# A hybrid Hyena and attention layer on one core: the RMSNorm sums taken by one product of ones with the squares

## The chip, the core and the metric

The kernel runs on one core of one Trainium2 chip. The metric is the device time of one execution in microseconds, the median over the runs. The engines are called PE (matrix products), DVE, ACT, POOL (three elementwise engines) and SP (which issues most DMAs).

## What is computed

One encoder layer on 512 positions of width 1024, all float32:

```python
def rmsnorm(x, g):
    return x * rsqrt(mean(x * x, axis=-1) + 1e-6) * g

x = x + 0.5 * swiglu(rmsnorm(x, ffn1_norm_g), ...)            # first FFN, width 2816
P = rmsnorm(x, mix_norm_g) @ w_in                             # 3*512 Hyena + 3*512 attention columns
y = concat(rmsnorm(hyena(P), g_h), rmsnorm(attention(P), g_a))
x = x + y @ w_out
x = x + 0.5 * swiglu(rmsnorm(x, ffn2_norm_g), ...)            # second FFN ("the second layer")
out = rmsnorm(x, final_norm_g)
```

So there are six norms: before the first FFN, before the mixer, on the Hyena output, on the attention output, before the second FFN, and the final one.

## The kernel before, in words

Activations lie transposed: a tile is 128 channels x 512 positions, so `g.x[0..7]` are the eight tiles of x, and a norm's sum runs over the partitions and over the tiles. Every large product is made of three matmuls of 128x128 by 128x512 (`mm3`, lines 146 to 148): high part by high part, low by high, high by low. The high and low parts of an activation tile are made by `gained`: ACT writes the high part times the norm's gain (tile `xh`, line 235), DVE the rest (`xl`, line 236). Weights are split in the same way by `wh` on ACT (line 188) and `wl` on DVE (line 194). A norm's factor does not go into the product's input; it multiplies the result, as a tile `rb` of 128x512 that holds 1/rms of each position in every row.

`SumSq.add` squares a tile on ACT (lines 249 and 252, tiles `ssq` and `sq`) and adds it to the sum on POOL (line 256). `SumSq.rstd` then turns the sum into `rb`: four products of 128 columns of the sum with a column of ones give the sums as 128x4 (`pc`, line 267); ACT takes the root (`std`, line 271, a table load ahead of it where another function was loaded), DVE the reciprocal (`rc`, line 273); DVE puts it on the diagonal of four 128x128 blocks (`dg`, line 276); PE multiplies by ones (`pb`, line 280); ACT copies that to SBUF (`rb`, line 285).

The stages: the first FFN (`ffn`, with its products `pgu` and `pd`); the mixer (`Mixer`: projections `pp` and `pv`, FFT-like products, elementwise work on DVE) and attention (`Attention`: `pqk`, softmax, `ppt`, `po`); the output projection in `Attention.out` (`pw`, eight output tiles, first with the Hyena half, then with the attention half); the second FFN; the final norm, which is worked off in two halves of 256 positions in `tail`. In the output projection's second half `evac` works off each tile d: `wt` = `pw` times the attention norm's `rb` (line 1047), x = x + `wt` (line 1049), the square of x through `done(d)`, and then `gained`, which gives `xh` and `xl` of the second FFN. The second FFN's first product needs all eight `xh` and `xl`.

The order on each engine is set twice. The code's streams are generators that a planner (`Merge`) lets run by estimated costs (`on_p`, `on_v`, `on_a`, `wait`); that gives the order in which instructions are written. The framework's own scheduler then puts them in the order in which each engine has them, within the dependencies and the ring buffers. The engines work in that order.

Of the kernel before, what the change touches and what calls it, by code (L numbers as in the profile page):

```python
# [18 lines left out]
P = 128  # L19
S = 512  # L20
# [46 lines left out]
def wait(ev):  # L67
    return "W", ev
# [172 lines left out]
class SumSq:  # L241
# [16 lines left out]
    def rstd(self, n, lag, res, m, ev=None, keep=True):  # L258

        g, nc = self.g, self.g.nc  # L260
        yield on_v(0.0, lag)
        yield on_p(1.7, ps=1)
        pc = psum(g, "pc")
        parts = [t for t in (self.acc, self.last) if t is not None]
        for b in range(4):
            for i, t in enumerate(parts):
                nc.tensor.matmul(pc[:, b:b + 1], t[:, b * P:(b + 1) * P], g.ones[:, 0:1],
                                 start=i == 0, stop=i == len(parts) - 1)
        yield on_v(0.7, 2.0)
# [12 lines left out]
        if keep:  # L282
            yield on_v(0.0, 0.9)
            res["rb"] = g.wp.tile([P, S], F32, tag="rb", name="rb", bufs=1)
            nc.scalar.copy(res["rb"], pb)
            m.free(ps=1)
        if ev is not None:
            m.fire(ev)

# [404 lines left out]
class Mixer:  # L694


    def __init__(self, g, m, hp, mid, xg):
        self.g, self.m, self.hp, self.mid, self.xg = g, m, hp, mid, xg
        self.conv = {}
        self.nev, self.gev = Event(), Event()  # L700
# [56 lines left out]
    def vproj(self):  # L757
# [15 lines left out]
        yield wait(self.nev)  # L773
# [101 lines left out]
class Attention:  # L875
# [146 lines left out]
    def out(self, done):  # L1022
# [15 lines left out]
        def evac(d, ps, last):  # L1038
# [11 lines left out]
            done(d)  # L1050
# [3 lines left out]
            self.x2[d] = gained(g, g.x[d], NG2 + d)  # L1054

        self.wev, self.x2 = Event(), [None] * DT
        for part in range(2):
            yg = self.yag if part else yhg
            for d in range(DT):
# [20 lines left out]
def body(ctx: ExitStack, tc: tile.TileContext, a: dict, out: bass.AP):  # L1080
# [83 lines left out]
    with pool("m1", **over) as hp:  # L1164
# [4 lines left out]
        m.spawn(ssm.rstd(D, LM, g.nm, m, mx.nev), 0)  # L1169
# [8 lines left out]
        def done(d):  # L1178
            ss2.add(g.x[d])

        m.spawn(at.prep_qk(), PQ)
        m.spawn(at.out(done), 20)
# [7 lines left out]
    with pool("f2", **over) as fp:  # L1190
# [12 lines left out]
        def tail(d, th, ps):  # L1203
# [3 lines left out]
            if d == DT - 2:  # L1207
                yield on_p(0.4, 0.0, ps=1)
# [12 lines left out]
            yield on_p(0.3)  # L1221
# [5 lines left out]
            yield on_v(0.3, 0.6)  # L1227
            std = g.wp.tile([P, 4], F32, tag="std", name="std", bufs=2)
# [142 lines left out]
```

## Time and profile before

| | us |
|---|---|
| runs | 1066.83, 1072.60, 1072.99 |
| median | 1072.6 |
| the profiled execution | 1065.19 |
| its span, first to last instruction | 1063.4 |
| mean granted clock of PE in it | 0.992 of full |

Rows of the profile give for each group of instructions the line, the engine, output<-inputs, partitions x elements and the count; a row of the timeline starts with its start and its duration, and ends with the idle time before it and what ended that. Instructions of an engine overlap somewhat, so a duration is about 0.08 us longer than the distance to the next one on DVE. A float32 product (`pc`, `pb`) is two instructions in the trace. PEclk is the granted clock as a share of full speed, where 1.00 is 2.4 GHz and 0.50 is 1.2 GHz.

### The profile page before, as it was taken

To read this page: it belongs to the slowest core of one execution; us is meant where nothing else is said; L and a number is where in the kernel's file an instruction comes from. 1 tells how busy PE (TensorE), PEld (TensorE's weight loads), DVE (VectorE), ACT (ScalarE), POOL (GpSimd) and SP (SyncE) were. 2 spreads that over 40 slices of the span, in tenths; PEclk is the share of its full clock that TensorE was granted. 3 is DMA by queue.
4 is the path that set the end of the run, shared out by engine and by line. 5 is a ranking of instruction groups with operands and counts; after the bars stand their busy time and mean duration, and the time that the engine had idled before them with its cause. 6 is when DMAs were issued, how large, how long until landed. Compare 5 with 4: busy or idle time off the path is not lost.

```text
span 1063.4 us, 12596 instructions
## 1 busy us (share of the span) xinstructions
PE 1046.8 (98%) x4962; PEld 860.2 (81%) x4962; DVE 609.3 (57%) x856; ACT 404.5 (38%) x598; POOL 45.1 (4%) x37
## 2 busy tenths in 40 slices
PE   9999999999999999999998999999999999999996
PEld 7877888888888888888886978688888888888886
DVE  5577646555666454879999355944444334444333
ACT  6433432234234342354348773432322122322341
POOL 4000000000000120000000100400000000000010
PEclk9999999999999999999999999899999999999998
DMA  6333324532264222334444303122222223333222
GB/s 213 118 132 104 124 89 137 163 97 90 90 192 156 89 98 70 98 100 144 163 131 153 94 1 99 55 84 99 99 99 100 86 93 99 99 100 99 85 74 80
DMA packets 43512, 114.25 MB, mean 107 GB/s; under 512 B 5081, under 2 KB 12313, under 8 KB 43452
## 3 DMA queue, kind: packets, MB, share of 16 engines
q1 hardware_dynamic: 41644, 111.30, 32.1%
q10 hardware_dynamic: 1808, 2.14, 0.6%
q8 instruction: 39, 0.64, 0.3%
q14 instruction: 21, 0.17, 0.0%
HBM read 106.08 MB, written 7.34 MB: 107 GB/s over the span
## 4 chain that ended last, share of the span: by engine, by line
PE 93%; DVE 3%; ACT 1%; DMA 1%; issue 1%; SPq 0%; DVEq 0%; ACTq 0%
PE pgu L148 15%; PE pgu L147 15%; PE pgu L146 15%; PE pd L146 8%; PE pd L147 8%; PE pd L148 8%; PE pp L146 3%; PE pp L148 3%; PE pp L147 3%; PE po L978 2%; PE pqk L994 1%; PE ppt L969 1%; PE pw L146 1%; PE pw L148 1%; PE pw L147 1%
## 5 line engine op out<-in xcount | busy, mean ns | idle before, releaser
L188 ACT ACTIVATE wh<-wr 128x1024 fp32r<-128x1024 f32 x159 | 168.5, 1060 | 431.9 <-PE pgu L147 139.7
L147 PE MATMUL pgu<-xl,wh 128*128 128x512 f32 x704 | 276.4, 393 | 2.8 <-DVE xl L236 2.7
L146 PE MATMUL pgu<-xh,wh 128*128 128x512 f32 x704 | 276.9, 394 | 0.6 <-ACT wh L556 0.6
L148 PE MATMUL pgu<-xh,wl 128*128 128x512 f32 x704 | 276.1, 392 | 0.2
L194 DVE TENSOR_TENSOR wl<-wr,wh 128x1024 fp32r<-128x1024 f32 x159 | 196.8, 1238 | 104.0 <-ACT wh L188 101.0
L147 PEld LDWEIGHTS pgu<-xl,wh 128*128 128x128 f32 x704 | 133.1, 189 | 33.4 <-DVE xl L236 4.8
L146 PEld LDWEIGHTS pgu<-xh,wh 128*128 128x128 f32 x704 | 132.8, 189 | 31.8 <-issue 2.9
L148 PEld LDWEIGHTS pgu<-xh,wl 128*128 128x128 f32 x704 | 133.1, 189 | 28.9 <-DVE wl L194 0.6
L146 PE MATMUL pd<-gh,wh 128*128 128x512 f32 (+1 forms) x374 | 143.2, 383 | 0.0
L147 PE MATMUL pd<-gl,wh 128*128 128x512 f32 (+1 forms) x374 | 142.7, 382 | 0.0
L148 PE MATMUL pd<-gh,wl 128*128 128x512 f32 (+1 forms) x374 | 142.7, 382 | 0.0
L307 DVE TENSOR_TENSOR u<-pgu,rb 128x512 f32<-128x512 f32 x44 | 30.4, 690 | 103.5 <-PE pgu L148 103.5
L256 POOL TENSOR_TENSOR ssq<-ssq,sq 128x512 f32<-128x512 f32 x31 | 44.5, 1434 | 992.9 <-ACT sq L252 899.8
L146 PEld LDWEIGHTS pd<-gh,wh 128*128 128x128 f32 x374 | 70.2, 188 | 15.1
L147 PEld LDWEIGHTS pd<-gl,wh 128*128 128x128 f32 x374 | 70.3, 188 | 15.0
L148 PEld LDWEIGHTS pd<-gh,wl 128*128 128x128 f32 x374 | 70.2, 188 | 15.0
L305 DVE TENSOR_TENSOR z<-pgu,rb 128x512 f32<-128x512 f32 x44 | 30.4, 691 | 65.3 <-PE pgu L148 65.3
L146 PE MATMUL pp<-xh,wh 128*128 128x512 f32 x128 | 50.1, 391 | 0.0
L148 PE MATMUL pp<-xh,wl 128*128 128x512 f32 x128 | 49.8, 389 | 0.0
L147 PE MATMUL pp<-xl,wh 128*128 128x512 f32 x128 | 49.8, 389 | 0.0
L319 DVE SCALAR_TENSOR_TENSOR x<-pd,x 128x512 f32<-128x512 f32 x30 | 20.7, 690 | 42.2 <-PE pd L148 42.2
L312 ACT ACTIVATE gh<-u 128x512 fp32r<-128x512 f32 x44 | 27.8, 632 | 23.9 <-DVE u L309 23.5
(207 smaller groups left out, 1223.2 us busy)
## 6 DMA issues: line engine op xcount, KB each, us to landing
wr<-w1u SPq DMA_DIRECT2D x22, 512.0 KB, 3.4
wr<-w1d SPq DMA_DIRECT2D x22, 512.0 KB, 3.3
wr<-w2g SPq DMA_DIRECT2D x22, 512.0 KB, 3.2
wr<-w2u SPq DMA_DIRECT2D x22, 512.0 KB, 3.4
wr<-w2d SPq DMA_DIRECT2D x22, 512.0 KB, 3.4
wr<-w1g SPq DMA_DIRECT2D x21, 512.0 KB, 3.3
wr<-win SPq DMA_DIRECT2D x16, 512.0 KB, 3.3
pe<-negb SPq DMA_DIRECT2D x32, 256.0 KB, 2.8
```

The source lines that it names most:

```text
L146: nc.tensor.matmul(ps, lh, rh, start=start, stop=False)
L147: nc.tensor.matmul(ps, lh, rl, start=False, stop=False)
L148: nc.tensor.matmul(ps, ll, rh, start=False, stop=stop)
L188: self.g.nc.scalar.activation(self.hi[i], self.raw[i], AF.Copy)
L194: self.g.nc.vector.tensor_tensor(out=self.lo[i], in0=self.raw[i], in1=self.hi[i].bitcast(F32), op=ALU.subtract)
L256: g.nc.gpsimd.tensor_tensor(out=self.acc, in0=self.acc, in1=sq, op=ALU.add)
L305: nc.vector.tensor_tensor(out=z, in0=pg, in1=rb, op=ALU.mult)
L307: nc.vector.tensor_tensor(out=u, in0=pu, in1=rb, op=ALU.mult)
L312: nc.scalar.activation(hi, u, AF.Copy)
L319: nc.vector.scalar_tensor_tensor(out=g.x[d], in0=ps, scalar=0.5, in1=g.x[d], op0=ALU.mult, op1=ALU.add)
L969: nc.tensor.transpose(ps[:, js], pe[:, js], g.ident)
L978: nc.tensor.matmul(self.po[pr][:, c * HD:(c + 1) * HD], t[:, j * P:(j + 1) * P], self.mx.v[j][:, h * HD:(h + 1) * HD], start=j == 0, stop= ...
```

## The change

`rstd` no longer goes through 128x4 sums. One product of the 128x128 tile of ones with the 128x512 sum of squares (and a second one for `last`, where there is one) gives the sums already in every row; ACT takes the root of 128x512 out of PSUM, DVE takes the reciprocal of 128x512 straight into `rb`. For the mixer's norm alone, whose factor is also needed by position (`rc`, 128x4, for the value projection), four transposes of 128 elements of `rb` follow on PE and a copy on ACT. The final norm does the same in halves of 256. In the output projection `done(d)` is gone: the eight squares are written by a stream of its own that waits for an event fired after the last `gained`, and the norm of the second FFN follows in the same stream. The attention norm's `rstd` is started ahead of the last four products of tile 0 instead of behind them.

```diff
-    def rstd(self, n, lag, res, m, ev=None, keep=True):
+    def rstd(self, n, lag, res, m, ev=None, cols=None):
         yield on_v(0.0, lag)
-        yield on_p(1.7, ps=1)
-        pc = psum(g, "pc")
         parts = [t for t in (self.acc, self.last) if t is not None]
-        for b in range(4):
-            for i, t in enumerate(parts):
-                nc.tensor.matmul(pc[:, b:b + 1], t[:, b * P:(b + 1) * P], g.ones[:, 0:1],
-                                 start=i == 0, stop=i == len(parts) - 1)
-        yield on_v(0.7, 2.0)
-        std = g.wp.tile([P, 4], F32, tag="std", name="std", bufs=2)
-        nc.scalar.activation(std, pc[:, 0:4], AF.Sqrt, bias=g.eps, scale=1.0 / n)
-        rc = g.wp.tile([P, 4], F32, tag="rc", name="rc", bufs=2)
-        nc.vector.reciprocal(rc, std)
-        dg = g.wp.tile([P, S], F32, tag="sq", name="dg", bufs=2)
-        for b in range(4):
-            nc.vector.tensor_scalar_mul(dg[:, b * P:(b + 1) * P], g.ident, rc[:, b:b + 1])
+        yield on_p(0.9 * len(parts), ps=1)
+        pb = psum(g, "pb")
+        for i, t in enumerate(parts):
+            nc.tensor.matmul(pb, g.ones, t, start=i == 0, stop=i == len(parts) - 1)
+        yield on_a(0.7)
+        std = g.wp.tile([P, S], F32, tag="sq", name="std", bufs=2)
+        nc.scalar.activation(std, pb, AF.Sqrt, bias=g.eps, scale=1.0 / n)
         m.free(ps=1)
-        yield on_p(0.9, ps=1)
-        pb = psum(g, "pb")
-        nc.tensor.matmul(pb, g.ones, dg, start=True, stop=True)
-        res["rc"], res["rb"] = rc, pb
-        if keep:
-            yield on_v(0.0, 0.9)
-            res["rb"] = g.wp.tile([P, S], F32, tag="rb", name="rb", bufs=1)
-            nc.scalar.copy(res["rb"], pb)
-            m.free(ps=1)
+        yield on_v(0.7, 0.4)
+        res["rb"] = g.wp.tile([P, S], F32, tag="rb", name="rb", bufs=1)
+        nc.vector.reciprocal(res["rb"], std)
         if ev is not None:
             m.fire(ev)
+        if cols is not None:
+            yield on_p(0.5, ps=1)
+            pc = psum(g, "pc")
+            for b in range(4):
+                nc.tensor.transpose(pc[:, b:b + 1], res["rb"][0:1, b * P:(b + 1) * P], g.ident[0:1, 0:1])
+            yield on_a(0.3)
+            res["rc"] = g.wp.tile([P, 4], F32, tag="rc", name="rc", bufs=2)
+            nc.scalar.copy(res["rc"], pc[:, 0:4])
...
             nc.vector.tensor_tensor(out=g.x[d], in0=g.x[d], in1=t, op=ALU.add)
-            done(d)
             if d >= 4:
                 yield wait(self.wev)
             yield on_v(0.7)
             self.x2[d] = gained(g, g.x[d], NG2 + d)
+            if d == DT - 1:
+                m.fire(self.xev)
...
                         yg[k] = gained(g, self.ya[k], NGA + k, vp)
+                        if k == CT - 1:
+                            m.spawn(self.ssa.rstd(C, LA, ra, m, aev), -1)
                     yield on_p(0.65, 0.0, ps=int(k == 0))
                     mm3(nc, ps, wblk(wc, 4 * (d % 2) + k), yg[k], k == 0, k == CT - 1)
-                if part and d == 0:
-                    m.spawn(self.ssa.rstd(C, LA, ra, m, aev), 0)
...
-        def done(d):
-            ss2.add(g.x[d])
+        def squares():
+            yield wait(at.xev)
+            for d in range(DT):
+                yield on_v(0.0, 1.4)
+                ss2.add(g.x[d])
...
             if d == DT - 2:
-                for b in range(2):
-                    bs = slice((2 * th + b) * P, (2 * th + b + 1) * P)
-                    nc.tensor.matmul(pc[th][:, b:b + 1], ss3.acc[:, bs], g.ones[:, 0:1],
-                                     start=b == 0, stop=False)
+                nc.tensor.matmul(pc[th][:, 0:CW], g.ones, ss3.acc[:, hs], start=True, stop=False)
...
-            for b in range(2):
-                nc.tensor.matmul(pc[th][:, b:b + 1], sq[d][:, b * P:(b + 1) * P],
-                                 g.ones[:, 0:1], start=False, stop=d == DT - 1 and b == 1)
+            nc.tensor.matmul(pc[th][:, 0:CW], g.ones, sq[d][:, 0:CW], start=False, stop=d == DT - 1)
...
-            nc.scalar.activation(std[:, 0:2], pc[th][:, 0:2], AF.Sqrt, bias=g.eps, scale=1.0 / D)
-            rc = g.wp.tile([P, 4], F32, tag="rc", name="rc", bufs=2)
-            nc.vector.reciprocal(rc[:, 0:2], std[:, 0:2])
-            dg = fp.tile([P, S], F32, tag="z", name="dg", bufs=2)
-            nc.vector.tensor_scalar_mul(dg[:, 0:P], g.ident, rc[:, 0:1])
-            nc.scalar.activation(dg[:, P:CW], g.ident, AF.Copy, scale=rc[:, 1:2])
-            pb = psum(g, "pb")
-            for b in range(2):
-                bs = slice(b * P, (b + 1) * P)
-                nc.tensor.matmul(pb[:, bs], g.ones, dg[:, bs], start=True, stop=True)
+            nc.scalar.activation(std[:, 0:CW], pc[th][:, 0:CW], AF.Sqrt, bias=g.eps, scale=1.0 / D)
+            pb = fp.tile([P, S], F32, tag="u", name="pb", bufs=2)
+            nc.vector.reciprocal(pb[:, 0:CW], std[:, 0:CW])
```

Where the instructions stand. First ACT, where the output projection's second half is worked off; `xh` are the high parts of the second FFN's input, `ssq` and `sq` the squares of the same tiles of x. Before:

```order
L249 ACTIVATE ssq_5560<-x0_65 128x512
L235 ACTIVATE xh_5583<-x0_65,cols_73 128x512
L252 ACTIVATE sq_5574<-x1_66 128x512
L235 ACTIVATE xh_5601<-x1_66,cols_73 128x512
L252 ACTIVATE sq_5611<-x2_67 128x512
L188 ACTIVATE wh_5617<-wr_5542 128x1024
L235 ACTIVATE xh_5635<-x2_67,cols_73 128x512
L252 ACTIVATE sq_5626<-x3_68 128x512
L235 ACTIVATE xh_5653<-x3_68,cols_73 128x512
```

And now:

```order
L235 ACTIVATE xh_5519<-x0_65,cols_73 128x512
L235 ACTIVATE xh_5529<-x1_66,cols_73 128x512
L249 ACTIVATE ssq_5645<-x0_65 128x512
L252 ACTIVATE sq_5659<-x1_66 128x512
L235 ACTIVATE xh_5565<-x2_67,cols_73 128x512
L252 ACTIVATE sq_5672<-x2_67 128x512
L188 ACTIVATE wh_5572<-wr_5511 128x1024
L235 ACTIVATE xh_5575<-x3_68,cols_73 128x512
L252 ACTIVATE sq_5690<-x3_68 128x512
L235 ACTIVATE xh_5617<-x4_69,cols_73 128x512
```

Each square has moved from just ahead of its tile's split to just behind it; the squares are not all behind the last split, although the numbers show that they were written after it.

Next ACT at the attention norm, a little earlier in the same stage, with the semaphores that each instruction waits for; `wh` are weights, `std` is the root. Before:

```order
L235 ACTIVATE yg_5482<-ya_5341,cols_73 128x512
L188 ACTIVATE wh_5506<-wr_5442 128x1024 [waits DMAHW3_49,DVE_49,PE_49]
L271 ACT_TABLE_LOAD
L271 ACTIVATE std_5521<-pc_5509,eps_74 128x4 [waits PE_49]
L285 COPY rb_5552<-pb_5547 128x512 [waits PE_49]
```

And now:

```order
L235 ACTIVATE yg_5453<-ya_5319,cols_73 128x512
L270 ACT_TABLE_LOAD [waits PE_49]
L270 ACTIVATE std_5474<-pb_5468,eps_74 128x512 [waits Pool_49]
L188 ACTIVATE wh_5482<-wr_5413 128x1024 [waits DMAHW3_49,DVE_49,PE_49]
L188 ACTIVATE wh_5526<-wr_5463 128x1024 [waits DMAHW4_49,DVE_49,PE_49]
```

The wait for PE has moved from the root to the table load ahead of it, and the two weight splits stand behind the root.

Last DVE in the same stage, from the reciprocal on; `wt` is the output projection times the norm, `xl` the low part. Before:

```order
L194 TENSOR_TENSOR wl_5540<-wr_5442,wh_5506 128x1024
L273 RECIPROCAL rc_5523<-std_5521 128x4
L276 TENSOR_SCALAR dg_5525<-ident_109,rc_5523 128x128 x4
L1047 TENSOR_TENSOR wt_5557<-pw_5459,rb_5552 128x512
L1047 TENSOR_TENSOR wt_5571<-pw_5489,rb_5552 128x512
L1049 TENSOR_TENSOR x0_65<-x0_65,wt_5557 128x512
```

And now:

```order
L274 RECIPROCAL rb_5485<-std_5474 128x512
L194 TENSOR_TENSOR wl_5509<-wr_5413,wh_5482 128x1024
L1045 TENSOR_TENSOR wt_5490<-pw_5430,rb_5485 128x512
L1045 TENSOR_TENSOR wt_5499<-pw_5460,rb_5485 128x512
L1047 TENSOR_TENSOR x0_65<-x0_65,wt_5490 128x512
L1047 TENSOR_TENSOR x1_66<-x1_66,wt_5499 128x512
```

The reciprocal now stands ahead of the weight's low part, which it holds up, and writes `rb` itself; the four diagonals are gone. From the first `wt` to the last `xl` DVE has the same 27 instructions as before (eight each of `wt`, x and `xl`, and three `wl`) in nearly the same order.

## Rows read from the trace of the kernel before

**Rows 1.** The page's first part: busy time, share of the span, instructions.
```profile
PE 1046.8 (98%) x4962; PEld 860.2 (81%) x4962; DVE 609.3 (57%) x856; ACT 404.5 (38%) x598; POOL 45.1 (4%) x37
```

**Rows 2.** Waits of PE: line, what ended them, total us, times, longest.
```profile
PE ppt L969 <- ACT pe L964: 3.0, 2, 2.7
PE pgu L147 <- DVE xl L236: 2.7, 3, 1.5
```

**Rows 3.** Busy time by stretch: us, PE, PEld, DVE, ACT, POOL, PEclk, DMA.
```profile
685.00:690.00 5.00, 4.72 (x11) 3.53 (x12) 5.00 (x5) 1.24 (x2) 3.43 (x2) 0.50 0.06 9
690.00:695.00 5.00, 5.00 (x17) 4.32 (x17) 1.57 (x7) 1.32 (x2) 0.00 (x0) 0.51 0.27 96
```

**Rows 4.** Timeline of PE at the start of the second FFN.
```profile
678.34 0.39 PE L146 MATMUL pgu<-xh,wh 128*128 128x512 f32 x1
678.57 0.40 PE L147 MATMUL pgu<-xl,wh 128*128 128x512 f32 x1
...
682.98 0.50 PE L147 MATMUL pgu<-xl,wh 128*128 128x512 f32 x1 [1.50 <-DVE xl L236]
...
685.28 0.79 PE L147 MATMUL pgu<-xl,wh 128*128 128x512 f32 x1 [0.89 <-DVE xl L236]
...
697.88 1.02 PE L280 MATMUL pb<-dg,ones 128*128 128x512 f32 x2
```

**Rows 5.** Timeline of DVE, end of the output projection.
```profile
666.14 1.29 DVE L1047 TENSOR_TENSOR wt<-pw,rb 128x512 f32<-128x512 f32 x2 [3.39 <-ACT rb L285]
...
673.85 1.60 DVE L1049 TENSOR_TENSOR x<-x,wt 128x512 f32<-128x512 f32 x1
...
682.18 0.74 DVE L236 SCALAR_TENSOR_TENSOR xl<-x,cols,xh 128x512 fp32r<-128x512 f32 x1
682.84 0.68 DVE L1049 TENSOR_TENSOR x<-x,wt 128x512 f32<-128x512 f32 x1
...
688.63 1.76 DVE L236 SCALAR_TENSOR_TENSOR xl<-x,cols,xh 128x512 fp32r<-128x512 f32 x1
```

**Rows 6.** Timeline of POOL in the same stretch.
```profile
673.60 1.30 POOL L256 TENSOR_TENSOR ssq<-ssq,sq 128x512 f32<-128x512 f32 x1 [2.02 <-ACT sq L252]
```

**Rows 7.** Groups of DVE by shape: busy us, mean ns.
```profile
L1047 DVE TENSOR_TENSOR wt<-pw,rb 128x512 f32<-128x512 f32 x8 | 5.2, 680 | 3.4 <-ACT rb L285 3.4
L276 DVE TENSOR_SCALAR dg<-ident,rc 128x128 f32<-128x128 f32 x20 | 4.4, 282 | 0.4
L273 DVE RECIPROCAL rc<-std 128x4 f32<-128x4 f32 x5 | 0.9, 176 | 5.2 <-ACT std L271 5.2
L1004 DVE RECIPROCAL dn<-dn 128x8 f32<-128x8 f32 x4 | 0.8, 200 | 2.4 <-ACT pe L964 2.4
L1231 DVE RECIPROCAL rc<-std 128x2 f32<-128x2 f32 x2 | 0.3, 166 | 3.0 <-ACT std L1229 3.0
```

**Rows 8.** The chain that ended last, by time: start, us, what.
```profile
407.96 0.79 PE pc L267 x8
...
413.00 0.86 PE pb L280 x2
...
659.11 1.68 PE pc L267 x16
...
690.34 1.50 PE pc L267 x8
```

**Rows 9.** Timeline of ACT at the attention norm.
```profile
660.00 1.28 ACT L271 ACT_TABLE_LOAD   x1
```

**Rows 10.** Groups of ACT by shape: a copy of 128x512 from PSUM.
```profile
L285 ACT COPY rb<-pb 128x512 f32<-128x512 f32 x5 | 2.9, 583 | 8.9 <-PE pb L280 8.8
```

**Rows 11.** Timeline of the last microseconds.
```profile
1054.34 0.42 ACT L1220 ACTIVATE sq<-x 128x256 f32<-128x256 f32 x1 [4.12 <-DVE x L1215]
1054.80 0.61 PE L1223 MATMUL pc<-ones,sq 128*128 128x1 f32 x4 [1.03 <-ACT sq L1220]
...
1057.18 2.08 DVE L1246 TENSOR_TENSOR o<-x,pb 128x256 f32<-128x256 f32 x6 [0.95 <-PE pb L1239]
```

More of the change, by code (lines that the diff above doesn't have):

```diff
@@ L287, in rstd @@
         if ev is not None:
             m.fire(ev)
+        if cols is not None:
[6 more added lines that the diff above has]
+            nc.scalar.copy(res["rc"], pc[:, 0:4])
+            m.free(ps=1)
+            m.fire(cols)
 def psum(g, name):
@@ L699, in __init__ @@
         self.conv = {}
-        self.nev, self.gev = Event(), Event()
+        self.nev, self.rev, self.gev = Event(), Event(), Event()
         self.gate = [Event(), Event()]
@@ L772, in vproj @@
                         kt == 0, kt == DT - 1)
-        yield wait(self.nev)
+        yield wait(self.rev)
         for b in range(4):
@@ L1020, in finish, with out @@
         self.m.fire(self.aev[pr])
-    def out(self, done):
+    def out(self):
         g, m, vp = self.g, self.m, self.vp
@@ L1054, in evac @@
             self.x2[d] = gained(g, g.x[d], NG2 + d)
+            if d == DT - 1:
+                m.fire(self.xev)
         self.wev, self.x2 = Event(), [None] * DT
+        self.xev = Event()
         for part in range(2):
@@ L1168, in body @@
         g.nm = {}
-        m.spawn(ssm.rstd(D, LM, g.nm, m, mx.nev), 0)
+        m.spawn(ssm.rstd(D, LM, g.nm, m, mx.nev, mx.rev), 0)
         for half in range(2):
@@ L1176, in body @@
         at = Attention(g, m, vp, mid, mx, a)
-        def done(d):
-            ss2.add(g.x[d])
+        def squares():
[3 more added lines that the diff above has]
+                ss2.add(g.x[d])
         m.spawn(at.prep_qk(), PQ)
-        m.spawn(at.out(done), 20)
+        m.spawn(at.out(), 20)
         m.spawn(at.stock(), HB)
@@ L1207, in tail @@
             if d == DT - 2:
[L1208 removed]
+                yield on_p(0.45, 0.0, ps=1)
                 pc.append(psum(g, "pc"))
[L1210 to L1213 removed]
+                nc.tensor.matmul(pc[th][:, 0:CW], g.ones, ss3.acc[:, hs], start=True, stop=False)
             yield on_v(0.35)
@@ L1220, in tail @@
             nc.scalar.activation(sq[d][:, 0:CW], x, AF.Square)
-            yield on_p(0.3)
-            for b in range(2):
-                nc.tensor.matmul(pc[th][:, b:b + 1], sq[d][:, b * P:(b + 1) * P],
-                                 g.ones[:, 0:1], start=False, stop=d == DT - 1 and b == 1)
+            yield on_p(0.45)
+            nc.tensor.matmul(pc[th][:, 0:CW], g.ones, sq[d][:, 0:CW], start=False, stop=d == DT - 1)
             if d < DT - 1:
                 return
-            yield on_v(0.3, 0.6)
-            std = g.wp.tile([P, 4], F32, tag="std", name="std", bufs=2)
-            nc.scalar.activation(std[:, 0:2], pc[th][:, 0:2], AF.Sqrt, bias=g.eps, scale=1.0 / D)
-            rc = g.wp.tile([P, 4], F32, tag="rc", name="rc", bufs=2)
-            nc.vector.reciprocal(rc[:, 0:2], std[:, 0:2])
-            dg = fp.tile([P, S], F32, tag="z", name="dg", bufs=2)
-            nc.vector.tensor_scalar_mul(dg[:, 0:P], g.ident, rc[:, 0:1])
-            nc.scalar.activation(dg[:, P:CW], g.ident, AF.Copy, scale=rc[:, 1:2])
-            yield on_p(0.9, 0.2, ps=1)
-            pb = psum(g, "pb")
-            for b in range(2):
-                bs = slice(b * P, (b + 1) * P)
-                nc.tensor.matmul(pb[:, bs], g.ones, dg[:, bs], start=True, stop=True)
+            yield on_a(0.4)
+            std = fp.tile([P, S], F32, tag="z", name="std", bufs=2)
+            nc.scalar.activation(std[:, 0:CW], pc[th][:, 0:CW], AF.Sqrt, bias=g.eps, scale=1.0 / D)
+            m.free(ps=1)
+            yield on_v(0.4, 0.2)
+            pb = fp.tile([P, S], F32, tag="u", name="pb", bufs=2)
+            nc.vector.reciprocal(pb[:, 0:CW], std[:, 0:CW])
             for c in range(DT // 2):
@@ L1251, in tail, with norm2 @@
                     out[2 * c:2 * c + 2, :, hs].rearrange("d p s -> p d s"), o)
-            m.free(ps=1)
         m.spawn(ffn(g, m, fp, at.x2, n2, nev, done2, tail), 1)
-        m.spawn(ss2.rstd(D, L2, n2, m, nev), 0)
+        def norm2():
+            yield from squares()
+            yield from ss2.rstd(D, L2, n2, m, nev)
+        m.spawn(norm2(), 0)
         m.run()
```

## The prediction

> **What bounds the kernel now.** I read the busy times first: PE works for 1046.8 of the 1063.4 us [rows 1], so a saving counts where it is PE's own work, or where PE stands still. Then the waits of PE [rows 2]: inside the kernel only two lines matter. PE waits once 2.7 us for the softmax (`ppt` on `pe`, in the mixer, where DVE is the late one), and 2.7 us in all for `xl`, the low parts of the second FFN's input. The second is dearer than it looks: in the stretches right behind it the granted clock is 0.50 and 0.51, that is 1.2 GHz [rows 3]. The timeline of PE gives its whole price [rows 4]: the second FFN's first two banks take 48 matmuls and run from 678.34 to 697.88, 19.5 us. At the distance of the first two rows (0.23 us) 48 matmuls are 11.1 us; the norm's `pc` in between took 1.50 [rows 8], against 0.79 for the same eight instructions at full clock. So this stage loses 19.5 - 11.1 - 0.8 = 7.6 us: about 2.7 standing (1.50 and 0.89 in the rows, the rest small), the other 4.9 at half clock.
>
> Why is `xl` late? DVE works from 666.14 to 688.63 + 1.76 = 690.39 without a gap [rows 5], on 27 instructions: eight `wt`, eight x, eight `xl`, three `wl`. Some take far longer than their twins: the x at 673.85 took 1.60, the one at 682.84 took 0.68. The first ran into POOL's add of a square, which started at 673.60 and lasted 1.30 [rows 6]; 673.60 + 1.30 = 674.90, and the x ended at 675.45, 0.55 later. So a DVE instruction with both inputs in SBUF stands still while POOL adds, and there are seven adds.
>
> **Part 1, the sums.** Per norm PE did `pc` 0.79 and `pb` 0.86 [rows 8]. Now it does one product of the same shape as `pb`, 0.86, so 0.79 goes. For the first FFN PE never waits around the norm, so 0.8 us is gained. For the mixer's norm four transposes with a 128x1 result come in. The trace has none; they cost nothing at best, and at most what the four products of that shape took, 0.79. I take 0.7 (the nearest row is `pc`), so the gain is 0.1. They wait for the reciprocal, but 19 matmuls (19 x 0.23 = 4.4 us) stand between them and the product, so that cover is enough up to a reciprocal of 3.7 (4.4 less a root of 0.58 [rows 10] and the hand-offs). For the Hyena norm 0.8 goes. The attention norm has two parts, 1.68 + 0.87 (as the other `pb`) against 2 x 0.86: 0.8. The second FFN's: 0.8, within the stage of part 3.
>
> **Part 2, the long reciprocal.** No reciprocal 512 wide stands in the trace. The narrow ones take 166 ns for 2 elements, 176 for 4 and 200 for 8 [rows 7]: 34 ns for 6 more, 5.7 ns each. Drawn on, 512 take 0.166 + 510 x 0.0057 = 3.1 us, and 256 take 1.6. From below the bound is an ordinary pass, 0.68 (`wt`); from above, with no fixed part at all, 200 / 8 x 512 = 12.8 us. I take 3.1, because three rows lie on one line. It replaces a reciprocal and four diagonals, 0.18 + 4 x 0.28 = 1.3 [rows 7], so DVE does 1.8 us more per norm, while ACT's copy of 0.58 becomes a root of the same width, and PE's second turn falls away. At the first FFN and the mixer the whole way to `rb` gets shorter and DVE was waiting there: no cost, and I book no gain, as nothing of PE hangs on it. At the Hyena norm DVE also has the last pair's softmax behind the reciprocal; ACT had the same queue ahead of it, so I take 0, with 1.8 as the far end.
>
> **Part 3, into the second FFN.** Take before's clock. `pc` of the attention norm started at 659.11, behind 24 matmuls of the second half. Now the first product stands behind 13 of them: 659.11 - 11 x 0.23 = 656.6; then 0.86, two matmuls, 0.86: done at 658.8. The table load, which had run beside PE (660.00, 1.28 [rows 9]), now waits for PE: 660.1. Root 0.6, reciprocal 3.1: 663.8. `wl` behind it 1.2: the first `wt` starts at 665.0 against 666.14, 1.1 earlier. Behind the load ACT has the root and two `wh`, behind the reciprocal DVE has that `wl`; PE wants them with the seventh tile, at about 671.8, over 6 us later, so nothing else is held up. From there DVE has the same 27 instructions. The squares now stand one place behind their tile's `xh`, not behind the last split, so POOL's adds still fall between them and still stop DVE. I therefore shift the row, not shorten it: the `xl` that came at 682.18 + 0.74 = 682.9 comes at 681.8 (or, if the adds fall worse, at 682.9 again). PE ends the projection 0.8 earlier, at 677.5, and wants that `xl` 13 matmuls later, at 680.5. It stands as long as before, and its clock will fall again. What is saved in the stage is the attention norm's 0.8 and `pc`, which at half clock cost 1.50; from 0.7 (the clock comes back at the same moment as before, and only the `pc` time turned into matmuls counts) to 2.7 (all of it and the earlier `xl`). I take 1.5. The second FFN's own `rb` comes later than before: its product now stands behind 96 matmuls, where `pb` stood behind 48, and the squares' sum is ready by then. PE fills a bank of PSUM in 24 matmuls, 5.6 us, and has eight; until `rb` comes, some 15 us later than before, three more are filled, so PE does not stand.
>
> **Part 4, the end.** From the start of the last `pc` to the first `o` it took 1057.18 - 1054.80 = 2.4 us [rows 11]. Now: a product half as wide as `pb`, about as long as that `pc` (0.6), a root 256 wide (0.42, as the square), a reciprocal of 1.6, hand-offs of 0.2: 2.8. That is 0.4 later. Of PE's own work in the two halves, six groups of small products and two `pb` become six products of 0.43; I book nothing for it.
>
> **Sum.** -0.8 - 0.1 - 0.8 - 1.5 + 0.4 = -2.8 us. On the profiled execution, 1065.2, that is 1062.4. The runs shown have their median 7.4 higher, at 1072.6, with one run near the profile; on the median it is 1069.8, say 1070.
>
> **Rivals.**
> First, slower: the reciprocal is longer than the line says, and decides at four places at once. Each us above 3.1 comes in full into the second FFN's start and the Hyena norm, by half at the end, and in full at the mixer beyond 3.7. With eight passes of 0.51 (an ordinary 0.68 less the 0.17 of the shortest) it is 0.17 + 4.1 = 4.3: +1.2 + 1.2 + 0.6 + 0.6 = 3.6, so 1073.4. At the bound of 12.8 it is +9.7 x 2.5 + 9.1 = 33, so 1103. It is slower than before from 4.1 on, and by over 1% from about 7. Against it: three rows on a line. The Trainium skill has a rule for this side: "VectorE: DVE Perf Modes", section "First, the fixed hardware budget", calls the reciprocal an iterative divide with a repeat count of 8. The narrow rows do not bear it out in full: by the same pass of 0.51 per 512, eight would be 8.0 ns per element, and they show 5.7.
>
> Second, faster: the squares do wait, and DVE is freed. A stopped instruction lost 0.9 (1.60 against 0.68); six adds less are 5 to 6 us, PE then never waits and keeps its clock: most of the 7.6 goes where I booked 1.5, so 1064. For it: POOL's rows. Against it: the order of ACT.
>
> Third: all as forecast, but the clock stays up. The 2.7 us wait in the mixer shows that a stand need not bring it down. It gives 4 more, 1066.
>
> Fourth, the mixer: DVE has 1.8 more in front of the stretch that ends in PE's 2.7 us wait, and the planner's order there is new. The wait grows by 1.8, and the clock falls there as it did behind `xl`, 4.9: 1076.5. Against it: `rb` itself is ready earlier.
>
> **How the numbers follow.** Forecast 0.55, first rival 0.10, second 0.10, third 0.12, fourth 0.13. The runs of before differ by 6 us among themselves, and a measurement tells about 1% (10.7 us) from no change. The range takes in the second rival with some spread of the runs below, 1061, and the fourth above, 1077. Over 1% faster needs the second rival and a low run, 0.06; over 1% slower needs the first rival far up or the fourth twice, 0.06; 0.88 lies between.
>
> **What would show it.** Right: reciprocals of 3.1 and 1.6 us; PE's `pb` at 0.86, 1.7 at the attention norm; first `wt` about 1 us earlier relative to the projection's end; POOL's adds still among the `xl`, DVE instructions of 1.2 to 1.8 there, PE waiting for `xl`, and a clock of 0.5 for some 10 us. Wrong: no wait there and a clock of 1.00, a table load beside PE, transposes that PE waits for, or a clock under 1 anywhere in the mixer.

## The result: 1057.6 us, 1.15% faster than before

The changed kernel's four executions took 1058.76, 1056.33, 1060.91 and 1056.21 us, median 1057.55; beside them the kernel before had a median of 1070.76. The ratio is 0.9885 [0.9843, 0.9928]. The forecast, 1070.0 with a range of 1061 to 1077, was too slow by 12 us. Twelve later executions of the same kernel gave 1058.6 and 0.9918 [0.9887, 0.9948], so the gain is nearer to 0.8 to 1.2%.

The profiled execution took 1058.76 (span 1057.0, mean granted clock 0.992, as before). First the busy times and PE's waits after the change, to hold against [rows 1] and [rows 2]:

```profile
PE 1036.7 (98%) x4900; PEld 853.3 (81%) x4900; DVE 622.3 (59%) x834; ACT 402.6 (38%) x592; POOL 46.1 (4%) x37
```

```profile
PE pgu L147 <- DVE xl L236: 4.2, 4, 2.2
PE ppt L967 <- ACT pe L962: 2.5, 2, 2.3
PE po L976 <- ACT pt L972: 1.8, 2, 1.5
```

PE is busy 10.1 us less, although it waits longer for `xl` (4.2 against 2.7) and has a new wait of 1.5, for `pt`. So the gain isn't a wait that went; PE's own work got shorter, by more than the products that the change takes out (0.8 per norm, six norms). Next the stretches at half clock (us, PE, PEld, DVE, ACT, POOL, PEclk, DMA); a stretch of 5 us with a PEclk of 0.65 has 2 x 0.35 x 5 = 3.5 us of it:

```profile
560.00:565.00 5.00, 4.08 (x19) 3.17 (x20) 5.00 (x11) 2.79 (x8) 1.73 (x1) 0.65 0.24 72
565.00:570.00 5.00, 5.00 (x30) 3.92 (x29) 4.05 (x9) 2.77 (x8) 0.00 (x0) 0.67 0.36 107
680.00:685.00 5.00, 1.61 (x5) 1.04 (x6) 5.00 (x7) 2.48 (x4) 2.75 (x3) 0.94 0.32 105
685.00:690.00 5.00, 5.00 (x18) 4.01 (x17) 3.38 (x4) 1.24 (x2) 1.96 (x2) 0.72 0.24 58
690.00:695.00 5.00, 5.00 (x24) 4.14 (x23) 1.79 (x2) 2.12 (x2) 0.00 (x0) 1.00 0.39 142
```

The second FFN's start has 3.4 us of half clock, where before had 10.2 [rows 3]; but 6.8 us now lie in the mixer, behind the wait for `pe`. The sum is 10.2 us in both profiled executions (the last microseconds apart), so these two can be compared directly: 1065.19 and 1058.76, 6.4 us apart. (The start differs a little: the same `pgu` row ahead of the first norm stands at 22.51 before and at 23.26 now, so from there to the end it is 7.2 us.)

The pieces of the change come next, against [rows 4] to [rows 10]. Groups of DVE in the changed kernel (busy us, mean ns):

```profile
L274 DVE RECIPROCAL rb<-std 128x512 f32<-128x512 f32 x5 | 16.8, 3352 | 8.4 <-ACT std L270 8.3
L1045 DVE TENSOR_TENSOR wt<-pw,rb 128x512 f32<-128x512 f32 x8 | 5.4, 680 | 0.0
L1232 DVE RECIPROCAL pb<-std 128x256 f32<-128x256 f32 x2 | 3.5, 1754 | 3.6 <-ACT std L1228 3.6
```

The root, in ACT's groups:

```profile
L270 ACT ACTIVATE std<-pb,eps 128x512 f32<-128x512 f32 x5 | 3.4, 689 | 4.4 <-PE pb L267 4.3
```

PE's sums in the chain (start, us), at the mixer's norm with the four transposes, and at the attention norm:

```profile
405.86 0.86 PE pb L267 x2
411.07 0.33 PE pc L281 x4
...
656.12 0.86 PE pb L267 x2
657.44 0.88 PE pb L267 x2
```

ACT's timeline at the attention norm, and below it POOL's and DVE's on the way into the second FFN:

```profile
658.38 1.28 ACT L270 ACT_TABLE_LOAD   x1 [3.77 <-PE pb L267]
659.68 0.69 ACT L270 ACTIVATE std<-pb,eps 128x512 f32<-128x512 f32 x1
```

```profile
682.17 1.58 POOL L256 TENSOR_TENSOR ssq<-ssq,sq 128x512 f32<-128x512 f32 x1 [1.97 <-ACT sq L252]
```

```profile
660.40 3.35 DVE L274 RECIPROCAL rb<-std 128x512 f32<-128x512 f32 x1 [4.24 <-ACT std L270]
...
664.75 1.27 DVE L1045 TENSOR_TENSOR wt<-pw,rb 128x512 f32<-128x512 f32 x2
...
681.27 0.74 DVE L236 SCALAR_TENSOR_TENSOR xl<-x,cols,xh 128x512 fp32r<-128x512 f32 x1
681.93 0.68 DVE L1047 TENSOR_TENSOR x<-x,wt 128x512 f32<-128x512 f32 x1
682.53 1.76 DVE L236 SCALAR_TENSOR_TENSOR xl<-x,cols,xh 128x512 fp32r<-128x512 f32 x1
```

PE's timeline there:

```profile
682.06 0.50 PE L147 MATMUL pgu<-xl,wh 128*128 128x512 f32 x1 [2.24 <-DVE xl L236]
...
684.35 0.80 PE L147 MATMUL pgu<-xl,wh 128*128 128x512 f32 x1 [1.32 <-DVE xl L236]
```

Most of this is as forecast: one product of 0.86 per part, the table load behind it, POOL's add still beside a DVE instruction that takes 1.76 instead of 0.74, and PE waiting for the same two `xl`. The sum of the forecast had -2.8 for it, not 6.4. What makes up most of the rest was found in the down products, of which the forecast says nothing. Here are two rows each of PE's timeline in the second FFN, first of the kernel before, then of the changed one:

```profile
840.01 0.39 PE L147 MATMUL pd<-gl,wh 128*128 128x512 f32 x1
...
843.51 0.40 PE L147 MATMUL pd<-gl,wh 128*128 128x512 f32 x1
```

And the changed kernel:

```profile
839.95 0.39 PE L148 MATMUL pd<-gh,wl 128*128 128x512 f32 x1
...
843.38 0.39 PE L148 MATMUL pd<-gh,wl 128*128 128x512 f32 x1
```

There are 15 matmuls from the first to the second row of each: 3.50 / 15 = 0.2333 us before, 3.43 / 15 = 0.2287 after, at full clock. Over all such pairs in `pd` (some 975 in each trace) the means are 0.2331 and 0.2290. The products into `pgu` take 0.227 in both (0.23 in [rows 4]). The change touches no down product; but it deletes the small tile `std` and places `rc` elsewhere, and by this every tile allocated behind them lies 64 bytes lower, with them `gh` and `gl`, the moving operands of `pd`, and the `yg` of `pw`.

### The profile page after: what moved, and what is told of

The parts are those of the page before. It is cut to its first block, busy times and chain, and to the rows that moved or that the text cites. A ratio compares the mean times of both kernels' runs of the same rounds, so it can differ in the third digit from the quotient of the medians.

```text
span 1057.0 us, 12423 instructions
## 1 busy us (share of the span) xinstructions
PE 1036.7 (98%) x4900; PEld 853.3 (81%) x4900; DVE 622.3 (59%) x834; ACT 402.6 (38%) x592; POOL 46.1 (4%) x37
## 4 chain that ended last, share of the span: by engine, by line
PE 94%; DVE 3%; ACT 1%; DMA 1%; issue 1%; SPq 0%; DVEq 0%; ACTq 0%
PE pgu L148 15%; PE pgu L147 15%; PE pgu L146 15%; PE pd L146 8%; PE pd L148 8%; PE pd L147 8%; PE pp L147 3%; PE pp L146 3%; PE pp L148 3%; PE po L976 3%; PE ppt L967 1%; PE pqk L992 1%; PE pw L146 1%; PE pw L148 1%; PE pw L147 1%; DVE x L1047 1%
```

## The experiments

Theory of the places: a matmul's distance depends on where its moving tile lies against its weights. Theory of the sums: the norms themselves gave it all. A third share may be the clock: executions of one kernel differ in their mean granted clock (0.978 to 0.995 in e10), and time goes with it. So beside the ratio the table gives the *reduced time*, time x mean granted clock, averaged over executions: the time less the most that half clock can have cost. It holds to about 2 us, too low where the clock was lowest. The first four executions of the changed kernel, which aren't in the table, have 1050.6. "Place" is the remainder by 256 of the addresses of the weights, and of `gh`, `gl`, `yg`; the distance of `pd` matmuls is from rows as above.

| kernel | places | pd, us | executions | median | ratio to before | clocks | reduced |
|---|---|---|---|---|---|---|---|
| before (beside the runs below) | 32, 160 | 0.2333 | 51 | 1069.2 | | 0.984-0.996 | 1057.2 |
| e1_before_shift | 32, 224 | 0.2333 | 6 | 1070.3 | 1.0011 [0.998, 1.0041] | 0.986-0.992 | 1057.6 |
| e12_before_addr32 | 32, 32 | 0.2267 | 6 | 1057.4 | 0.9903 [0.9869, 0.9936] | 0.986-0.995 | 1050.4 |
| e4_before_shift_squares_late | 32, 224 | 0.2333 | 6 | 1065.7 | 0.9977 [0.995, 1.0004] | 0.989-0.993 | 1057.9 |
| e2_after_unshift | 32, 160 | 0.2333 | 6 | 1067.1 | 0.999 [0.9946, 1.0033] | 0.980-0.995 | 1053.7 |
| e10_after_again | 32, 96 | 0.229 | 12 | 1058.6 | 0.9918 [0.9887, 0.9948] | 0.978-0.995 | 1049.7 |
| e3_after_squares_early | 32, 96 | 0.229 | 6 | 1065.1 | 0.9939 [0.9899, 0.9978] | 0.986-0.997 | 1051.0 |
| e5_after_addr32 | 32, 32 | 0.2267 | 7 | 1063.6 | 0.9919 [0.988, 0.9959] | 0.978-0.992 | 1046.3 |
| e11_after_all96 | 96, 96 | 0.2267 | 6 | 1056.0 | 0.9879 [0.9844, 0.9915] | 0.980-0.996 | 1048.3 |
| e6_after_fill | 32, 96 | 0.229 | 6 | 1061.2 | 0.990 [0.9869, 0.9932] | 0.987-0.995 | 1050.4 |
| e7_after_pairs_by_tile | 32, 96 | 0.229 | 6 | 1054.7 | 0.9888 [0.9841, 0.9934] | 0.981-0.997 | 1048.0 |
| e8_all | 32, 32 | 0.2267 | 6 | 1054.9 | 0.9847 [0.9817, 0.9876] | 0.991-0.997 | 1047.0 |
| e9_all_fill2 | 32, 32 | 0.2267 | 6 | 1057.9 | 0.988 [0.9852, 0.9909] | 0.991-0.997 | 1049.8 |
| e13_all_fill3 | 32, 32 | 0.2267 | 6 | 1050.2 | 0.9827 [0.9804, 0.9851] | 0.996-0.998 | 1046.9 |

### The places

Five kernels change nothing but the number of buffers of a small tile, or its size:

```diff
# e1, e12: the kernel before, both lines of std with 4 (e1) or 6 (e12) buffers
-        std = g.wp.tile([P, 4], F32, tag="std", name="std", bufs=2)
+        std = g.wp.tile([P, 4], F32, tag="std", name="std", bufs=4)
# e2, e5: the changed kernel, rc with 4 (e2) or 8 (e5) buffers
-            res["rc"] = g.wp.tile([P, 4], F32, tag="rc", name="rc", bufs=2)
+            res["rc"] = g.wp.tile([P, 4], F32, tag="rc", name="rc", bufs=4)
# e11: as e5, and
-    g.warm = warm = g.wp.tile([P, 1], F32, tag="warm", name="warm")
+    g.warm = warm = g.wp.tile([P, 17], F32, tag="warm", name="warm")[:, 0:1]
```

> The kernel before with one edit that computes nothing: the small std tile (16 bytes a partition) gets four buffers instead of two, so that everything allocated behind it, above all gh and gl (the moving operands of the down products) and yg, lies 64 bytes higher, at 96 instead of 32 beyond a multiple of 128, as in the changed kernel. Address theory: most of the gain that the norm sums don't explain is the down products reading from better placed tiles; their start-to-start time over 835 to 880 us falls from 0.2318 to about 0.228 us, and with some 1300 such matmuls the kernel is 4 to 6 us faster than before (ratio 0.994 to 0.996), with all norm chains as long as before. Sums theory: the whole gain is the norms' work; nothing changes here (ratio 0.998 to 1.002, start-to-start time 0.2318).

> The changed kernel with the small rc tile given four buffers instead of two, which puts gh, gl, z, u and yg back to the addresses they have in the kernel before (32 beyond a multiple of 128). Address theory: the down products' start-to-start time returns from 0.2283 to 0.2318 us over 835 to 880 us, and 4 to 6 us of the gain go: ratio to before 0.992 to 0.995. Sums theory: nothing changes against the changed kernel, ratio 0.9885 within its interval.

The first was a miss: 64 bytes higher is not like 64 bytes lower, 0.2333 and no gain. The second hit by its distance: with the old places the changed kernel has 0.2333 again. Its ratio, 0.999, lies above the 0.992 to 0.995 that were expected, as three of its six executions have clocks of 0.980 to 0.984. Its profiled execution has the same two stretches of half clock as that of the changed kernel, 6.8 and 3.4 us, and took 1062.49: 3.7 us slower than the changed kernel, and 2.7 faster than before (3.5 and 3.7 when the starts are taken off: its `pgu` row stands at 23.47). The remainder that counts had to be that by 256, and perhaps the distance between the two tiles:

> The changed kernel with eight buffers for the small rc tile, so that gh, gl and yg lie 32 beyond a multiple of 256, like xh, xl, wh and wl (they lie at 160 in the kernel before, at 224 in the first experiment and at 96 in the changed kernel). Theory of the distance: what counts is how far the moving tile lies from the weights, and at equal places a down product takes 0.2267 us from start to start like the products from xh and xl; against 0.2289 in the changed kernel that is 1300 x 0.0022 = 3 us faster than it at the same granted clock (about 1053.5 at a clock of 0.992 to 0.993, ratio to before 0.984 to 0.988). Theory that 96 was merely a lucky place: 0.229 to 0.233 us, same as or slower than the changed kernel by up to 5 us.

> The changed kernel with a tile of 68 bytes for the one of 4 that lies ahead of wh, wl, xh and xl, and eight buffers for rc: the weights and xh and xl lie 96 beyond a multiple of 256 instead of 32, and gh, gl and yg at 96 as in the changed kernel. Theory that the distance between weights and moving tile counts: all products take 0.2267 us from start to start, those of pd too, and time x clock is 1046 to 1048 like with all of them at 32. Theory that the place of the moving tile alone counts (32 good, 96 a little worse): pd stays at 0.2289 and the products from xh and xl rise to 0.2289 as well, time x clock 1053 to 1056.

> The kernel before with six buffers for std instead of two, which puts gh, gl and yg 32 beyond a multiple of 256 with everything else as before. Theory of the distance: down products at 0.2267 instead of 0.2318 us, time x clock 1057 - 6 to 7.5 = 1049.5 to 1051, about what the changed kernel has, without any of its change; ratio to before 0.993 to 0.995. If the places matter only together with the new sums: no change, 0.998 to 1.002.

All three hit by their distances. (By time, e5's profiled execution has the two stretches of half clock of the changed kernel's and took 1054.99, 3.8 us less; its median and its ratio are higher than expected, at lower clocks. e11's reduced time is 0.3 over what was expected, and e12's ratio of 0.990 is better than it.) PE's timeline with moving tiles and weights both at 96 (e11):

```profile
839.97 0.39 PE L147 MATMUL pd<-gl,wh 128*128 128x512 f32 x1
...
843.37 0.39 PE L147 MATMUL pd<-gl,wh 128*128 128x512 f32 x1
```

The same with both at 32 and the old sums (e12):

```profile
839.90 0.39 PE L147 MATMUL pd<-gl,wh 128*128 128x512 f32 x1
...
843.30 0.39 PE L147 MATMUL pd<-gl,wh 128*128 128x512 f32 x1
```

3.40 / 15 = 0.2267 in both: 96 is as good as 32 when the weights lie there too. By the difference of the remainders: 0 gives 0.2267, 64 gives 0.229, 128 and 192 give 0.2333. This is shown for `pd` and `pw`. The mixer's products of `xh` and `xl` with the weight tile `we`, which lies at 224, fit: 0.230 in the mean where the two are 64 apart, and 0.233 in e11, where they are 128 apart. A few filter products (`pf`), whose two tiles both lie at 224, don't: they take 0.230 or more. With 990 matmuls of this kind in `pd` (330 in each of its three groups) the change's accidental step from 128 to 64 is worth 990 x 0.0043 = 4.3 us, and the step to 0 would be 6.5; `pw` adds 192. Measured by reduced time: e2 to the changed kernel 4.0, before to e12 6.8. e12 has no part of the change and gains nearly as much as the changed kernel's 7.5.

### The squares

> The changed kernel with the eight squares of the second layer's sum put back to where they were before (each right behind its x add, inside the split loop); sums and addresses as in the changed kernel. Theory that the deferral carries part of the gain: ACT has 0.6 us a tile more between the splits, xl of tile 4 comes 1 to 2 us later, PE's first product of the second layer waits that much longer and the half clock behind it lasts nearer to the 10 us it has before; 3 to 6 us slower than the changed kernel (ratio 0.991 to 0.995). Theory that the deferral does nothing (POOL's adds lie between the splits in both, and VectorE's x add sets the pace): within 0.2% of the changed kernel, ratio 0.987 to 0.990.

> The kernel before with the 64 byte shift of the first experiment and the deferred squares of the change; norm sums as before (products with one column, reciprocal 4 wide, diagonal). Against the first experiment it shows the deferral alone, and against the changed kernel the sums alone at equal addresses. Deferral carries part: 3 to 6 us under the first experiment. Deferral does nothing: within 2 us of it. Sums theory: the changed kernel stays 3 us or more under this one, since the norm chains of both feed-forward layers are 2 us shorter there.

```diff
# e3: the changed kernel, and in the split loop again
             nc.vector.tensor_tensor(out=g.x[d], in0=g.x[d], in1=t, op=ALU.add)
+            done(d)
# e4: the reverse, in e1
```

By their medians e3 lies 6.5 us over the changed kernel and e4 4.6 under e1, but this is clock: four executions of e3 have 0.986 and two 0.997. Reduced, the squares' place is worth 1.3 us in the one pair and -0.3 in the other: nothing that can be told from zero. POOL's adds stand between the splits in both. Whether the squares' place has a part in how often the clock falls isn't settled: the mean clocks are 0.990 for e3 and 0.989 for e10, but 0.989 for e1 and 0.992 for e4. And e4 doesn't show the sums at equal places, as its expectation has it: by 256 its tiles lie at 224, those of the changed kernel at 96.

### The waits and the clock

e6 and e9 put products of ones with ones, which nobody reads, in front of PE's two waits in the mixer; e7 takes the first gate and up products of the second FFN tile by tile; e8 is e5, e6 and e7 together, and e9 and e13 add to e8:

```diff
# e6, e8, e9, e13
             ps = psum(g, "ppt")
+            if pr == 0 and b == 0 and e == 0:
+                for _ in range(9):
+                    nc.tensor.matmul(ps[:, 0:P], g.ones, g.ones, start=True, stop=True)
# e7, e8, e9, e13: for the first f of the second FFN
+                wa = g.w.take()
+                wb = (g.w.hi[g.w.i], g.w.lo[g.w.i])
+                for k in range(DT):
...
+                    for ps, wc in zip(pgu, (wa, wb)):
+                        mm3(nc, ps, wblk(wc, k), xg[k], k == 0, k == DT - 1)
# e13; e9 has pr == 1 and range(12)
             yield on_p(0.9)
+            if pr == 3 and b == 0 and e == 0:
+                for _ in range(7):
+                    nc.tensor.matmul(self.po[pr][:, 0:HD], g.ones, g.ones[:, 0:HD], start=True, stop=True)
```

> The changed kernel with nine products of ones with ones (128 columns, results overwritten by the transposes that follow) put ahead of the first transpose of exponentials, where PE waits 2.3 us for ACT with nothing to do (558.7 to 560.9 us). They compute nothing that is used. Clock theory: the half clock that follows this wait in some executions and not in others (0, 6.8 or 20.5 us of it) goes, the granted clock is 0.995 or more in every execution, and the times gather at the lowest of the changed kernel: 1054 to 1057 us, spread under 2 us. Rival, the clock falls there for another reason or later instead: spread and clocks as in the changed kernel (0.986 to 0.995), or slower by the products' own 1 to 2 us.

A miss. The wait for `pe` is gone (2.5 us to 0.2), and so is the half clock behind it, but in the profiled execution 13.7 us of half clock stand behind the next wait, the 1.5 us for `pt` (and 6.8 at the second FFN's start). That they moved there because the first wait was filled isn't shown: the profiled executions of e3, e7 and e11 have 3.4, 10.2 and 10.2 us of half clock at that second place although they also have over 20 at the first. Its stretches:

```profile
556.00:561.00 5.00, 4.95 (x39) 3.70 (x37) 5.00 (x9) 4.72 (x11) 1.73 (x1) 1.00 0.56 209
610.00:615.00 5.00, 4.83 (x35) 3.23 (x33) 4.12 (x8) 4.89 (x8) 0.00 (x0) 1.00 0.00 0
615.00:620.00 5.00, 3.43 (x18) 3.20 (x19) 5.00 (x13) 3.63 (x10) 1.28 (x1) 0.74 0.00 0
620.00:625.00 5.00, 5.00 (x25) 4.78 (x23) 2.86 (x5) 4.25 (x9) 0.00 (x0) 0.50 0.00 0
```

> The changed kernel with the first gate and up products of the second feed-forward layer taken tile by tile (gate with tile 0, up with tile 0, gate with tile 1 ...) instead of one after the other, so that PE has six matmuls for each tile that the split loop delivers, not three. Theory that PE's wait for xl there is real lost time (2.2 + 1.3 + 0.7 us) and the cause of the half clock behind it (3.4 us at half speed, so 1.7 lost): the wait falls under 1.5 us, the half clock there goes, 3 to 5 us faster than the changed kernel at the same clock elsewhere. Rival: the split loop sets the end of this stretch whatever PE does in it (the tile 7 split ends at 690 us in both), and the wait comes back behind tile 7: gain under 1 us.

PE's wait for `xl` in e7:

```profile
PE pgu L147 <- DVE xl L236: 1.0, 3, 0.5
```

Its stretches at the second FFN's start:

```profile
676.00:680.00 4.00, 4.00 (x19) 3.26 (x19) 4.00 (x8) 2.84 (x5) 0.00 (x0) 1.00 0.37 131
680.00:685.00 5.00, 5.00 (x24) 4.10 (x23) 5.00 (x5) 2.82 (x4) 3.78 (x2) 1.00 0.10 13
685.00:690.00 5.00, 4.48 (x20) 3.35 (x18) 5.00 (x7) 2.42 (x5) 1.66 (x1) 1.00 0.24 92
```

A hit: the wait for `xl` falls from 4.2 to 1.0, and the clock is 1.00 where it was 0.94 and 0.72. (A wait of 1.1 for `wl` comes instead, at 690.58, and no half clock behind it.) At clocks of 0.993 it took 1054.3 and 1055.1, the changed kernel at 0.992 about 1058.5, which is 2.7 us more when the 0.001 of clock (1.06 us) is taken off. The mixer's half clock it leaves alone: 23.9 us behind the wait for `pe` and 10.2 behind that for `pt` in the profiled execution.

> All three edits at once: gh, gl and yg at the places of the weights, the nine filling products in the mixer, the second layer's first pair tile by tile. If each theory holds the parts add: 3 + 2 to 5 + 3 to 5 us under the changed kernel, so 1046 to 1050 us, ratio to before 0.977 to 0.982. If only the addresses hold: 1053 to 1055.

Half a hit: two executions at 1049.8 and 1050.1, the other four at 1054.9 to 1056.3 with clocks of 0.991 to 0.993; in the profiled one of these the 13.7 us behind the wait for `pt` were left. The median, 1054.9, lies where the expectation had it if only the places held.

> The kernel with all three edits (places of gh, gl and yg; nine filling products; the second layer's first pair tile by tile) and twelve more filling products of 64 columns ahead of the first po product of the second pair of heads, where PE waits 1.5 us behind the Hyena norm's reciprocal. Clock theory: the 13.7 us of half clock that remained behind that wait go, granted clock 0.996 to 0.997 in every execution, all times 1049 to 1051 us, ratio to before 0.981 to 0.983. Rival (the half clock there comes from something else): clocks 0.991 to 0.997 and 1050 to 1056 us as with the three edits, or the products cost their own 1.3 us.

A miss of the edit: the products stood at 581 us, where PE had other work, so the wait stayed and their own 2.8 us were paid (reduced 1049.8 against 1047.0).

> The changed kernel as it is, again, since its four executions had clocks of 0.990 to 0.995 and those of its near copies 0.978 to 0.997. If the first four were drawn from the same spread, its median rises to 1058 to 1062 us (ratio 0.990 to 0.993), and time x clock stays at 1050 to 1051.5 in every execution, 6 to 7 under the kernel before (1056 to 1058). If the change itself keeps the clock up: 1056 to 1059 again.

The first held for the clocks (0.978 to 0.995) and for the ratio. The median, 1058.6, lies in both ranges and tells nothing; the reduced times spread further than expected, from 1046.5 to 1051.8. By the clocks, the change doesn't keep the clock up.

> As the kernel with all three edits, with seven filling products of 64 columns (14 passes, 1.5 us) ahead of the first po product of the fourth pair of heads, where PE waits 1.5 us (614.8 to 616.3 us there), instead of the twelve that stood at the second pair. Theory that the half clock there follows PE's wait: it goes, granted clock 0.996 to 0.997 in every execution, all times 1049 to 1051 us, ratio to before 0.981 to 0.983. Rival: it stays in four of six executions (clock 0.991 to 0.993) or moves to the next wait, 1054 to 1056 us as with the three edits.

A hit: six executions between 1049.4 and 1050.6 with clocks of 0.996 to 0.998, and in the profiled one half clock nowhere but in the last microseconds. A wait of 1.3 for `wl` remains at the second FFN's start. PE's timeline at the place:

```profile
614.68 0.66 PE L983 MATMUL ppt<-ident,pe 128*128 128x128 f32 x4 [0.22 <-ACT pe L975]
615.17 1.75 PE L993 MATMUL po<-ones 128*128 128x64 f32 x14
616.76 0.28 PE L983 MATMUL ppt<-ident,pe 128*128 128x128 f32 x1
616.87 1.08 PE L995 MATMUL po<-v,pt 128*128 128x64 f32 x8
```

The stretches around both waits and at the second FFN's start:

```profile
560.00:565.00 5.00, 4.22 (x32) 3.27 (x34) 5.00 (x10) 2.78 (x7) 0.35 (x1) 1.00 0.35 105
...
615.00:620.00 5.00, 4.76 (x43) 4.46 (x41) 5.00 (x13) 4.89 (x13) 1.28 (x1) 1.00 0.00 0
...
680.00:685.00 5.00, 4.57 (x21) 3.47 (x20) 4.81 (x6) 1.52 (x3) 2.16 (x3) 1.00 0.00 2
```

This kernel beats both, 0.9827 of the time before.

## Why the prediction was wrong

**The sum held in size, in part by luck.** The forecast was -2.8 us, 1062.4 on the profiled execution. With the old places (e2) and the same 10.2 us of half clock, the profiled execution took 1062.49. That it agrees so closely is luck: it started 0.96 us later (23.47 against 22.51), and from there on the change is worth 3.7. Reduced, it is worth 1057.2 - 1053.7 = 3.5 at the old places, and at the best ones, against e12's 1050.4, between 2.1 (e11) and 4.1 (e5). Its terms:

- *First FFN, -0.8.* As booked: from that `pgu` row to the first `pp` it takes 379.78 us before and 378.83 in e2, 376.62 in e12 and 375.91 in e5, so 0.95 and 0.71 less.
- *Mixer's transposes, 0.7 taken.* 0.33, so 0.4 more gained than booked. *Hyena norm, -0.8, and its far end of 1.8 that was taken as 0.* A wait came, 1.5 for `pt` where before had 0.4 at most there, but the rows don't put it on DVE's reciprocal, which runs from 615.82 for 3.35. PE waits for a copy on ACT, and ACT works from 612.97 to that copy without a gap, the root between two table loads among it:

```profile
613.80 1.28 ACT L270 ACT_TABLE_LOAD   x1
615.80 1.28 ACT L962 ACT_TABLE_LOAD   x1
619.52 0.57 ACT L972 COPY pt<-ppt 128x512 f32<-128x512 f32 x1
620.14 1.10 PE L976 MATMUL po<-v,pt 128*128 128x64 f32 x8 [1.52 <-ACT pt L972]
```

- *The mixer as a whole* came out well: from the norm product to the first `pgu` of the second FFN e5 needs 270.2 us and e12 269.7, with 6.8 us of half clock in e5 and none in e12, so some 3 us less at equal clock. Booked for this stretch were -1.7, the attention norm's -0.8 among them; beyond the 0.4 of the transposes, where the rest comes from isn't shown.
- *Reciprocals of 3.1 and 1.6.* 3.35 and 1.75: (3352 - 1754) / 256 = 6.2 ns per element, the line of the narrow rows said 5.7. The first rival's 4.3 is out. The Trainium skill's repeat count of 8 ("VectorE: DVE Perf Modes", "First, the fixed hardware budget"), read as eight of the passes of 0.51 us taken there, would be 8.0 ns; the trace doesn't bear that out at 512 either.
- *Second FFN's start, -1.5.* The adds stand between, and the same `xl` is late, as argued. From the attention norm's product to the first `wt` it takes 8.6 us (664.75 - 656.12; 8.4 forecast). The first `pgu` comes 12.0 behind that `wt` (676.70) where it was 12.2 before [rows 4, 5], so the sign "first `wt` about 1 us earlier relative to the projection's end" didn't come, and PE waits longer, 4.2 against 2.7. From the first `pgu` to the first `pd`, e5 needs 126.4 us and e12 127.1, both with 3.4 us of half clock: -0.7, and with the attention norm's 0.8, counted in the stretch before, that is the -1.5.
- *The end, +0.4.* From the last `pc` (1047.73) to the first `o` (1050.76) 3.0 against 2.4 [rows 11]: +0.6. PE's own work in the halves, booked as nothing, gave some of it back: from the first `pd` of the second FFN to the last `pc` it takes 244.3 us in e12 and 243.7 in e5.

**The step that failed** is a term that the sum doesn't have. It adds up instructions that go, come or move, and lets every other matmul keep its distance; where it counts matmuls it takes "the distance of the first two rows (0.23 us)", and the down products stand in it at nothing. Their distance was a second number, 0.2333, that the trace of before showed and the forecast didn't read, and the change made it 0.2287 by deleting a tile of 16 bytes. That was worth 3.5 us between the profiled executions of e2 and the changed kernel (starts taken off) and 4.0 by reduced time, more than the whole sum.

**A second step failed, and on the median it counts for more:** "The runs shown have their median 7.4 higher". The forecast carried these 7.4 us between before's profiled execution and the median of three over to the changed kernel, whose median lies 1.2 below its profiled execution: 8.6 of the 12.4 us by which 1070.0 was too slow. What differs is the clock of the executions. Of before, 51 executions have a median of 1069.2, only 4.0 above the profiled one. The medians 1069.2 and 1058.6 are 10.6 apart, the reduced times 7.5, of which 3.5 are the change and 4.0 the places. The other 3 follow where each kernel's executions happened to fall between 0.978 and 0.996; that the change caused it isn't shown, since its near copies e2, e3 and e5 have medians at lower clocks.

**The rivals.** The third (the clock stays up) and the fourth (it falls in the mixer) both came in part in the profiled execution: 3.4 us instead of 10.2 at the second FFN, 6.8 in the mixer, and the sum the same. But the wait for `pe` didn't grow as the fourth had it (2.5 against 3.0), and e1, with the old sums, has 20.5 us of half clock at that place and 3.4 at the second FFN. So this pattern goes with the execution. The second rival (the squares really wait) is out by POOL's rows and by e3 and e4.

## What to carry to other kernels

When an edit adds or removes a small tile, compare the addresses of all later tiles, and see in the trace whether equal matmuls still follow each other at the same distance; here the down products were fastest with moving tiles and weights at the same remainder by 256 bytes, and it costs one padding tile. Compare executions with the same granted clock, or times multiplied by it, before looking for a cause of a per cent. Where PE's waits can't be removed, ordering its work by arrival (e7) or filling the wait with idle products in exactly that place (e8 to e13: 4.7 us of median) kept the clock up behind that wait, and with all three done the spread went too; in a place where PE is busy such products cost their own length (e9).

## What the runs showed of the hardware

- The distance from one 128x512 matmul of `pd` to the next was 0.2267, 0.229, 0.2333 and 0.2333 us at full clock for moving tiles 0, 64, 128 and 192 bytes (by 256) from the weights. It goes little with the other engines' work: in the kernel before, distances during most of which none of DVE, ACT and POOL worked are 0.2330 in the mean, and those with DVE and ACT both at work 0.2335. The Trainium skill says that PE's reads of SBUF never wait on another engine ("SBUF — State Buffer", "SBUF: two separate sides"); by these two means the trace agrees. But the runs show that PE's own two operands are not free of each other, by up to 3%. Why isn't shown.
- Half clock stood behind waits of PE of 1.5 to 2.6 us in some executions and not in others. Behind the wait for `pe` it was gone in the profiled executions of all four kernels that filled it (e6, e8, e9, e13); only with the wait for `pt` filled too and the second FFN's products in order of arrival (e13) did all six executions keep 0.996 or more.
- A reciprocal 512 wide takes 3.35 us on DVE, five times an ordinary product of that size (0.68).
